# Second-layer modulation summed on VectorE, and the convolution branch ahead of the gating branch

## The chip, the cores and the metric

The kernel runs on one core of a Trainium2 chip. Its time is device microseconds of one execution. Three executions took 2710.41 us in the median (2707.55 to 2712.38).

## What is computed

Two transformer blocks follow each other, both with two layers, 256 tokens of width 1024, all in float32.

Part 1, per layer: a mixer with three attention branches (each gated by a sigmoid and projected, then summed), a layer norm, cross attention to a memory of 256 rows, a layer norm, a SwiGLU feed-forward network (FFN) of width 2816, a layer norm.

Part 2, per layer, works on those 256 tokens and, in its first layer, on 256 context tokens beside them. Its modulation and the merge of its branches are, cut from the reference:

```python
silu_c, silu_cc = jax.nn.silu(c), jax.nn.silu(c_ctx)            # one vector of 1024 each
mod_lat = (silu_c @ ada_w[l] + ada_b[l])[:, None, :]            # ada_w[l]: 1024 x 6144
mod_ctx = silu_cc @ ada_w[l] + ada_b[l]
sh1, sc1, g1, sh2, sc2, g2 = jnp.split(mod_lat, 6, axis=-1)
csh1, csc1, cg1, csh2, csc2, cg2 = jnp.split(mod_ctx, 6, axis=-1)
h = modulate(rmsnorm(x, norm1_g[l]), sh1, sc1)                  # also for the context
z = h @ w_in[l]
y_a = spatial_gating(gelu(z_u), layernorm(gelu(z_v)))           # gating branch
y_b = rmsnorm(differential_attention(z_q, z_k, z_v))            # attention branch
y_c = gb * dwconv3(gc * xin, cw)                                # convolution branch
m = g_a * (y_a @ wa) + g_b * (y_b @ wb) + g_c * (y_c @ wc)      # g: sigmoid gates of h
x = x + g1 * (m @ wo)
x = x + g2 * conv_ffn(modulate(rmsnorm(x, norm2_g[l]), sh2, sc2))
```

In the last layer only the keys and values of the context are used, so of the context's modulation only `csh1` and `csc1` (the first 2048 columns) count there.

## The kernel before

Each weight matrix is split into a high and a low part, and a product takes three matmuls (high by high, high by low, low by high). `wload` (line 83) fetches 512 KB of weights by SP's queue into one of three `raw` tiles; ScalarE writes the high part into one of four `whi` tiles (L91), VectorE the low part into one of four `wlo` tiles (L92). `gemm_N` (line 100) streams 512 weight columns against 128 tokens at a time, matmuls L96 to L98; `gemm_T` (line 141) streams the tokens, matmuls L171. Accumulators of both come from four PSUM banks (`acc_g`); two more (`acc_m`) serve transposes and small products, and one pair (`acc_s`) the attention scores.

The program is written as Python loops that are unrolled. A planner orders each engine's instructions when the kernel is built: it takes the earliest instruction in program order that its own cost estimates hold for ready, with a tile free for it. Later work is thus moved into gaps of earlier work, and each engine then runs its list strictly as laid out. SP holds all loads and stores in one list. `behind` (line 76) adds order to that: while `fence["D"]` is set, the conversions on VectorE come after the fenced instruction. `post_norm` sets it to the last operation of the norm behind cross attention (`ln_xa_g`, line 421), whose function also calls a `filler` between the norm and the transposes of its result (line 423).

Modulation: `ada_steps` (line 684) computes both streams of both layers of part 2 in 48 steps, three groups of 2048 columns per layer and eight steps of 128 rows per group. A step loads two raw tiles of 512 KB (no conversion) and issues four float32 matmuls of 32 columns by 512 (L696), which appear as eight records; a group ends with the addition of the bias on VectorE (L704) and stores to DRAM (`modd`), from where `mod_row` reads single rows later. Of the 48 steps, 8 are the filler of the norm behind cross attention in each layer of part 1, 8 that of the norm behind the first FFN; 11 stand in each FFN's loop, one per iteration (line 817), and one behind each FFN (line 840). The filler of the norm behind the mixer is `mem_k`, the key projection of the memory (96 matmuls L171). Tiles of the ring `kv_tile` (8 of 512 KB) serve keys, values and modulation weights.

Part 2, per layer: key, value and query GEMMs; eight attention heads in two groups of four (scores L1046, transposes L347, products L1067, transposes of keys and queries L1024); the GEMM of the gating values with `emit_sv` (line 1120), which takes the slot `mT` for its result `sv`; `gating` with its own products (L1142); `merge(0)`, which begins the sum `mT`; `head_norm`, which scales the attention output; `convolution`; `merge(2)`; then, in memory that the attention released, the transposes of the attention output and `merge(1)`. In layer 1 the convolution stands before `merge(0)`. In layer 0 the tile tags double: keys and queries of heads 0 to 3 use the slot of `mT`, those of heads 4 to 7 the slot `y` of the branch results.

Of the kernel before, what the change touches and what calls it, by code (L numbers as in the profile page):

```python
# [12 lines left out]
ALU = mybir.AluOpType  # L13
# [14 lines left out]
def body(ctx: ExitStack, tc: tile.TileContext, A: dict, out: bass.AP):  # L28
# [12 lines left out]
    cfg = {"narrow": True, "pt": 3}  # L41
# [31 lines left out]
    def v3(ap, n):  # L73
        return ap.rearrange("p (a b) -> p a b", b=n)
# [8 lines left out]
    def wload(kt, n, srcs):  # L83
# [8 lines left out]
        behind("D", V.tensor_sub(lo[:, :kt * n], raw[:, :kt * n], hi[:, :kt * n]))  # L92
        return v3(hi[:, :kt * n], n), v3(lo[:, :kt * n], n)
# [128 lines left out]
    ident = cst.tile([128, 128], F32, name="ident")  # L222

# [43 lines left out]
    def kv_tile():  # L267
        return xo.tile([128, 1024], F32, name="kv", tag="kv", bufs=8)
# [385 lines left out]
    def mem_k(l):  # L654
        kx = v3(kv_tile(), 256)
        evac_T(kx, gemm_T(memT, 256, A["xa_w_kv"][l], 0, 4))
        return kx
# [13 lines left out]
    def ada_prep():  # L671
# [40 lines left out]
    def ada(n, P, raw_tile):  # L712
        cfg["ada"] = (P, raw_tile)
        for _ in range(n):
            next(ada_it)

# [46 lines left out]

    for l in range(L):
        mfin = mixer(l, xT)
        with tc.tile_pool(name="xa", bufs=1, reuse_waits="tile") as P:
            mem = {}

            def fill_k(l=l):
                mem["k"] = mem_k(l)  # L770
            x, xT = post_norm(P, pair(mfin), A["w_mix_out"][l], 8, x, "ln_mix_g", "ln_mix_b", l, filler=fill_k)
            kx = mem["k"]
# [24 lines left out]
            for qb in range(2):  # L797
                ops = v3(bank_m(), 128)
                for h in range(4):
                    for kt in range(2):  # L800
# [5 lines left out]
                              filler=lambda: ada(8, P, lambda: P.tile([128, 1024], F32, name="adar", tag="adar", bufs=8)))  # L806
        with tc.tile_pool(name="ffn", bufs=1, reuse_waits="tile") as P:
# [4 lines left out]
            for (cb, nb, gps), (_, _, ups) in zip(gg, uu):  # L812
# [4 lines left out]
                ada(1, P, kv_tile)  # L817
# [22 lines left out]
            ada(1, P, kv_tile)  # L840
# [12 lines left out]
    cfg.update(narrow=False, pt=2)  # L853
    def md_tile(P):
        return lambda: P.tile([128, 1024], F32, name="md", tag="md", bufs=7)
# [32 lines left out]
    for l in range(L):  # L888
# [7 lines left out]
        with tc.tile_pool(name="mix2", bufs=1, reuse_waits="tile") as P:  # L896
# [220 lines left out]

            sv = P.tile([128, 4, 512], F32, name="sv", tag="mT", bufs=1)

            def emit_sv(tb, ps):  # L1120
                gv = gelu2(ps)
                st = small()[:, :6]
                mv = small()[:, :2]
                V.bn_stats(out=st, in_=gv)
                V.bn_aggr(out=mv, in_=st)
                rs = rsqrt(mv[:, 1:2], 1, 1.0, 4e-6)
                V.tensor_scalar(out=sv[:, tb, :], in0=gv, scalar1=mv[:, 0:1], scalar2=rs, op0=ALU.subtract, op1=ALU.mult)
            gemm_N(hT, qtbs, W, 512, 512, emit_sv, tail=2)

# [3 lines left out]
            def gating():  # L1133
# [18 lines left out]
            def merge(n, y, Wb, kt):  # L1152
                proj = gemm_T(y, ntok, Wb, 0, 8, kt=kt)
                gate = gemm_T(hT, ntok, W, 5632 + n * 1024, 8)
                for (cb, nb, gps), (_, _, pps) in zip(gate, proj):
# [3 lines left out]
                    if n == 0:  # L1159
# [42 lines left out]
            with tc.tile_pool(name="yb", bufs=1, reuse_waits="tile") as PB:  # L1202
                yb = PB.tile([128, 2, 8, ntok], F32R, name="yb", tag="yb")
                for tb in qtbs:
# [7 lines left out]
                merge(1, pair(yb), A["w_br_b_2"][l], 8)  # L1212
            mfin = wide_xT()
            for cb in range(8):
                split((mfin[0][:, cb, 0:ntok], mfin[1][:, cb, 0:ntok]), mT[:, cb, :], scale=0.5)
        with tc.tile_pool(name="ffn2", bufs=1, reuse_waits="tile") as P:
# [24 lines left out]
            for npart in ((12, 10) if ns == 2 else (22,)):  # L1241
# [6 lines left out]
                for (cb, nb, gps), (_, _, ups) in zip(gg, uu):  # L1248
# [8 lines left out]
            if l == 0:  # L1257
                hT2 = modulated(P, 1, (1, 0), "norm1_g_2", 0)

# [58 lines left out]
```

## Time and profile before

| | |
|---|---|
| median of three executions | 2710.41 us (2707.55 to 2712.38) |
| profiled execution | 2707.87 us, span 2706.1 us |
| TensorE (PE) matmuls | busy 2639.3 us, 98% |
| VectorE (DVE) | busy 1698.3 us, 63% |
| ScalarE (ACT) | busy 1245.0 us, 46% |
| mean granted TensorE clock | 0.991 of full |
| DMA | 419.16 MB, mean 155 GB/s |

A busy TensorE isn't TensorE at its peak: its matmuls are pipelined and the ends of records are modelled, so neighbouring records overlap, and what one costs is read from the distance between starts. The granted clock is the mean over a stretch of a clock with two levels. A line number such as L92 is that of the listing; where a helper issues an instruction, the line is the helper's. Part 1 runs from 0 to about 1160 us, layer 0 of part 2 to about 2145 us, layer 1 to the end.

### The profile page before, as it was taken

The numbers are of one execution on the slowest core, as the hardware profiler recorded it, in microseconds if no ns is written. First come the engines' busy times: TensorE is split into PE (matmuls) and PEld (weight loads), VectorE is DVE, ScalarE is ACT, GpSimd is POOL, SyncE is SP. The second block draws the span as 40 slices with busy tenths as digits, with TensorE's granted clock in tenths as the row PEclk, the third lists the DMA queues.
The fourth block names the chain that finished last, engine by engine and source line by source line (L and its number), as shares of the span: only waits on it lengthen the run. The fifth ranks groups of instructions, "written<-read, shape, count | busy, mean of one in ns | idle before, by whom it ended". The sixth has DMA issues, their size and how long they took to land.

```text
span 2706.1 us, 40562 instructions
## 1 busy us (share of the span) xinstructions
PE 2639.3 (98%) x15961; PEld 2238.6 (83%) x15961; DVE 1698.3 (63%) x3227; ACT 1245.0 (46%) x1983; POOL 24.6 (1%) x12
## 2 busy tenths in 40 slices
PE   9999999999999999999989999999999999999999
PEld 8889879868988698777767888788888877899997
DVE  6666754546666656678656433675365787766884
ACT  5655434326554444346653222344143356644663
POOL 0010000000010000000000000000000000000000
PEclk9999999999999999999989999999999999999999
DMA  7545877765457687531112333443232233366564
GB/s 223 159 133 179 279 265 244 237 209 161 141 158 265 228 277 244 184 97 55 55 55 71 101 94 94 157 130 96 86 117 93 84 103 108 110 190 208 169 185 153
DMA packets 416838, 419.16 MB, mean 155 GB/s; under 512 B 19708, under 2 KB 348760, under 8 KB 416648
## 3 DMA queue, kind: packets, MB, share of 16 engines
q1 hardware_dynamic: 416648, 416.58, 49.1%
q8 instruction: 125, 2.05, 0.3%
q14 instruction: 65, 0.53, 0.1%
HBM read 415.36 MB, written 1.16 MB: 154 GB/s over the span
## 4 chain that ended last, share of the span: by engine, by line
PE 87%; DVE 6%; ACT 3%; DMA 2%; issue 1%; POOL 0%; POOLq 0%; SPq 0%; ACTq 0%; DVEq 0%
PE acc_g L171 50%; PE acc_g L98 9%; PE acc_g L96 9%; PE acc_g L97 9%; PE acc_m L696 2%; PE acc_m L347 2%; DVE wlo L92 1%; PE acc_m L1067 1%; ACT whi L91 1%; PE acc_s L1046 1%; PE acc_m L378 1%; ACT ap L1057 1%; DVE ap L1062 1%; PE acc_m L231 0%; PE acc_s L471 0%
## 5 line engine op out<-in xcount | busy, mean ns | idle before, releaser
L92 DVE TENSOR_TENSOR wlo<-raw,whi 128x1024 fp32r<-128x1024 f32 (+3 forms) x644 | 782.2, 1216 | 642.5 <-ACT whi L91 635.8
L171 PE MATMUL acc_g<-xT,whi 128*128 128x256 f32 (+1 forms) x5440 | 1165.8, 311 | 1.6 <-ACT xT L209 1.2
L91 ACT CAST whi<-raw 128x1024 fp32r<-128x1024 f32 (+3 forms) x644 | 667.6, 1038 | 924.3 <-PE acc_g L171 499.7
L171 PEld LDWEIGHTS acc_g<-xT,whi 128*128 128x128 f32 x5440 | 882.5, 189 | 85.5 <-issue 23.4
L171 PE MATMUL acc_g<-xT,wlo 128*128 128x256 f32 (+1 forms) x2720 | 836.5, 310 | 0.0
L171 PEld LDWEIGHTS acc_g<-xT,wlo 128*128 128x128 f32 x2720 | 511.3, 189 | 30.0 <-issue 2.1
L96 PE MATMUL acc_g<-whi,xT 128*128 128x512 f32 (+2 forms) x792 | 313.4, 397 | 0.9 <-ACT xT L209 0.7
L98 PE MATMUL acc_g<-whi,xT 128*128 128x512 f32 (+2 forms) x792 | 312.6, 395 | 0.0
L97 PE MATMUL acc_g<-wlo,xT 128*128 128x512 f32 (+2 forms) x792 | 312.5, 395 | 0.0
L96 PEld LDWEIGHTS acc_g<-whi,xT 128*128 128x128 f32 x792 | 150.3, 190 | 35.7 <-issue 4.7
L98 PEld LDWEIGHTS acc_g<-whi,xT 128*128 128x128 f32 x792 | 150.4, 190 | 33.6 <-issue 5.1
L97 PEld LDWEIGHTS acc_g<-wlo,xT 128*128 128x128 f32 x792 | 150.5, 190 | 32.1 <-issue 4.4
L171 PE MATMUL acc_g<-y,whi 128*128 128x256 f32 (+1 forms) x640 | 135.4, 305 | 0.2 <-ACT y L212 0.2
L171 PEld LDWEIGHTS acc_g<-y,whi 128*128 128x128 f32 x640 | 102.8, 188 | 7.0 <-ACT y L212 0.9
L97 PE MATMUL acc_g<-wlo,hid 128*128 128x512 f32 x264 | 104.3, 395 | 0.0
L98 PE MATMUL acc_g<-whi,hid 128*128 128x512 f32 x264 | 104.3, 395 | 0.0
L96 PE MATMUL acc_g<-whi,hid 128*128 128x512 f32 x264 | 104.3, 395 | 0.0
L171 PE MATMUL acc_g<-y,wlo 128*128 128x256 f32 (+1 forms) x320 | 97.4, 304 | 0.0
L349 ACT COPY pt<-acc_m 128x512 f32<-128x512 f32 (+1 forms) x92 | 50.3, 547 | 62.6 <-PE acc_m L347 62.3
L1057 ACT ACTIVATE ap<-acc_s,sa,rq 128x512 f32<-128x512 f32 (+1 forms) x96 | 67.2, 706 | 20.4 <-DVE sa L1054 20.3
L96 PE MATMUL acc_g<-whi,hT 128*128 128x512 f32 x176 | 69.8, 397 | 0.0
L97 PE MATMUL acc_g<-wlo,hT 128*128 128x512 f32 x176 | 69.5, 395 | 0.0
(325 smaller groups left out, 2929.9 us busy)
## 6 DMA issues: line engine op xcount, KB each, us to landing
raw<-in_w_in_dram SPq DMA_DIRECT2D x200, 512.0 KB
raw<-in_ffn_w_gu_dram SPq DMA_DIRECT2D x88, 512.0 KB
raw<-in_ffn_up_dram SPq DMA_DIRECT2D x88, 512.0 KB
kv<-in_ada_w_dram SPq DMA_DIRECT2D x64, 512.0 KB
raw<-in_ffn_w_down_dram SPq DMA_DIRECT2D x44, 512.0 KB
raw<-in_ffn_down_dram SPq DMA_DIRECT2D x44, 512.0 KB
adar<-in_ada_w_dram SPq DMA_DIRECT2D x32, 512.0 KB
raw<-in_w_in_dram SPq DMA_DIRECT2D x64, 256.0 KB
```

The costliest lines, as they stand in the source:

```text
L91: behind("A", SC.copy(hi[:, :kt * n], raw[:, :kt * n]))
L92: behind("D", V.tensor_sub(lo[:, :kt * n], raw[:, :kt * n], hi[:, :kt * n]))
L96: PE.matmul(acc, sh, mh, start=first, stop=False)
L97: PE.matmul(acc, sh, ml, start=False, stop=False)
L98: PE.matmul(acc, sl, mh, start=False, stop=last)
L171: PE.matmul(acc[:, j, cut], blocks[kk][wi], xT[xi][:, kk, cut], start=n == 0, stop=n == len(steps) - 1)
L347: PE.transpose(p3[:, j, :], s2d[:, j * 128:(j + 1) * 128], ident)
L349: SC.copy(pt[:, :n * 128], ps[:, :n * 128])
L378: PE.matmul(ops[64 * e:64 * e + 64, i, :], pv(hsets[e][i], kt), pts[e][:, i * nkt + kt, :], start=kt == 0, stop=kt == nkt - 1)
L696: PE.matmul(acc[32 * j:32 * j + 32, :], scT[:, k, :], raw[:, jj * 512:(jj + 1) * 512], start=k == 0, stop=k == 7)
L1046: PE.matmul(pss[a_], QT[r, qi, tb * 128:tb * 128 + 128], KT[r, ki, k0:512], start=i == 0, stop=i == 2)
L1057: SC.activation(out=p[a_], in_=pss[a_], func=AF.Exp, scale=rq[tb][:, a_, h:h + 1], bias=nm[:, a_:a_ + 1], accum_out=sums[:, a_:a_ + 1])
```

## The change

1. `ada_steps` runs over layer 0 of part 2 alone: 24 steps. The calls `ada(1, ...)` in and behind the FFNs go. The fillers are: `mem_k(0)`, then `mem_k(1)` behind cross attention in layer 0 (its result in another tile, `xc`), 8 steps behind the FFN of layer 0, 8 steps behind the mixer of layer 1, 8 steps behind its cross attention.
2. Layer 1's modulation is computed by the new generator `ada_last` during layer 0 of part 2. It advances by one step every second `wload` (`cfg["rate"]` = 0.5) in the merges and gating, and in the FFN. A step loads 512 KB into a tile of the ring `raw`, multiplies it by the condition value of its row (per partition), and adds it to a 128x1024 accumulator, all on VectorE: four operations of 128x512 where both streams are needed (first 2048 columns, two row blocks per step), one of 128x1024 elsewhere (one row block per step). After 4 or 8 steps, 48 in all, the chunk is split into high and low, summed over the partitions by four matmuls against a matrix with one column of ones, copied by ScalarE and stored.
3. In part 2 the order is convolution, `merge(2)`, `head_norm`, release of the attention's memory, gating (its value GEMM included, `sv` now in that memory), `merge(0)`, transposes, `merge(1)`.

```diff
@@ wload
+        cfg["due"] += cfg["rate"]
+        if cfg["due"] >= 1:
+            cfg["due"] -= 1
+            next(ada_l1, None)
         return v3(hi[:, :kt * n], n), v3(lo[:, :kt * n], n)
@@ mem_k
-        kx = v3(kv_tile(), 256)
+        kx = v3(kv_tile() if l == 0 else xc.tile([128, 1024], F32, name="xc", tag="xc", bufs=2), 256)
@@ ada_prep
+        V.tensor_copy(cond, scT[:, :, 0:2])
+        zo = xo.tile([128, 129], F32, name="zo")
+        V.memset(zo, 0.0)
+        V.memset(zo[:, 1:2], 1.0)
+        SC.copy(pick, zo)
@@ ada_steps
-        for l in range(L):
+        for l in (0,):
@@ new
+    def ada_last():
+        W = A["ada_w_2"][1]
+        bias = A["ada_b_2"][1:2]
+        for c0 in (0, 512, 1024, 1536, 2048, 3072, 4096, 5120):
+            both = c0 < 2048
+            acc = cfg["acc"]()
+            V.memset(acc, 0.0)
+            for j in range(2):
+                c = c0 if both else c0 + 512 * j
+                nc.sync.dma_start(out=acc[0:1, j, :], in_=bias[:, c:c + 512])
+            for k in range(0, 8, 2 if both else 1):
+                raw = wp.tile([128, 1024], F32, name="raw", tag="raw", bufs=3)
+                if both:
+                    nc.sync.dma_start(out=v3(raw, 512), in_=W[k * 128:(k + 2) * 128, c0:c0 + 512].rearrange("(k p) n -> p k n", p=128))
+                    for kk in range(2):
+                        for s in range(2):
+                            V.scalar_tensor_tensor(out=acc[:, s, :], in0=raw[:, kk * 512:kk * 512 + 512],
+                                                   scalar=cond[:, k + kk, s:s + 1], in1=acc[:, s, :], op0=ALU.mult, op1=ALU.add)
+                else:
+                    nc.sync.dma_start(out=raw, in_=W[k * 128:(k + 1) * 128, c0:c0 + 1024])
+                    a2 = acc.rearrange("p a b -> p (a b)")
+                    V.scalar_tensor_tensor(out=a2, in0=raw, scalar=cond[:, k, 0:1], in1=a2, op0=ALU.mult, op1=ALU.add)
+                if k < (6 if both else 7):
+                    yield
+            hi = v3(wp.tile([128, 1024], F32R, name="whi", tag="whi", bufs=4), 512)
+            lo = v3(wp.tile([128, 1024], F32R, name="wlo", tag="wlo", bufs=4), 512)
+            SC.copy(hi, acc)
+            V.tensor_sub(lo, acc, hi)
+            ps = bank_m()
+            for j in range(2):
+                for i, part in enumerate((hi, lo)):
+                    PE.matmul(ps, pick[:, 1 - j:129 - j], part[:, j, :], start=j + i == 0, stop=j + i == 2)
+            SC.copy(acc[0:2, 0, :], ps[0:2, :])
+            dst = modd[1, :, c0:c0 + 512] if both else modd[1, 0:1, c0:c0 + 1024].rearrange("o (j n) -> (o j) n", j=2)
+            nc.sync.dma_start(out=dst, in_=acc[0:2, 0, :])
+            yield
@@ part 1, each layer
-            x, xT = post_norm(P, pair(mfin), A["w_mix_out"][l], 8, x, "ln_mix_g", "ln_mix_b", l, filler=fill_k)
+            x, xT = post_norm(P, pair(mfin), A["w_mix_out"][l], 8, x, "ln_mix_g", "ln_mix_b", l,
+                              filler=(lambda: fill_k(0)) if l == 0 else lambda: ada(8, P, kv_tile))
...
-                              filler=lambda: ada(8, P, lambda: P.tile([128, 1024], F32, name="adar", tag="adar", bufs=8)))
+                              filler=(lambda: fill_k(1)) if l == 0 else lambda: ada(8, P, adar_tile))
...
-                ada(1, P, kv_tile)
...
-            ada(1, P, kv_tile)
@@ part 2, each layer (gating now holds emit_sv and its GEMM, with sv = PB.tile(...))
-            ya = gating()
             mT = P.tile([128, 8, ntok], F32, name="mT", tag="mT", bufs=1)
-            if ns == 1:
-                yc = convolution()
-            merge(0, pair(ya), A["w_br_a_2"][l], 4)
+            yc = convolution()
+            if l == 0:
+                cfg["rate"] = 0.5
+            merge(2, pair(yc), A["w_br_c_2"][l], 4)
             for tb in qtbs:
                 head_norm(tb)
-            if ns == 2:
-                yc = convolution()
-            merge(2, pair(yc), A["w_br_c_2"][l], 4)
             att.close()
             with tc.tile_pool(name="yb", bufs=1, reuse_waits="tile") as PB:
                 yb = PB.tile([128, 2, 8, ntok], F32R, name="yb", tag="yb")
+                ya = gating(PB)
+                merge(0, pair(ya), A["w_br_a_2"][l], 4)
...
                 merge(1, pair(yb), A["w_br_b_2"][l], 8)
+            cfg["rate"] = 0
@@ FFN of part 2, in the loop over hidden blocks
+                    if l == 0:
+                        cfg["rate"] = 0.5
...
+                if b0 > 0:
+                    cfg["rate"] = 0
```

The first merge to run (now `merge(2)`) writes `mT`, the others add to it.

## Rows read from the trace of the kernel before

**Rows 1.** Page: engine, busy us, share of the span, instructions
```profile
PE 2639.3 (98%) x15961; PEld 2238.6 (83%) x15961; DVE 1698.3 (63%) x3227; ACT 1245.0 (46%) x1983; POOL 24.6 (1%) x12
```

**Rows 2.** Windows: length; busy PE, PEld, DVE, ACT, POOL; clock; DMA share; GB/s
```profile
1400.00:1420.00 20.00, 13.18 (x57) 9.93 (x58) 7.69 (x22) 9.62 (x24) 0.00 (x0) 0.56 0.00 0
1560.00:1580.00 20.00, 20.00 (x88) 16.28 (x87) 7.94 (x9) 5.62 (x7) 0.00 (x0) 1.00 0.26 80
2340.00:2360.00 20.00, 16.49 (x125) 16.27 (x126) 14.61 (x30) 11.74 (x21) 0.00 (x0) 0.91 0.16 44
```

**Rows 3.** Chain of waits, attention of layer 0: start, us, what
```profile
1380.22 0.44 PE acc_s L1024 x4
...
1383.41 3.92 PE acc_g L171 x16
1387.34 0.55 PE acc_s L1046 x5
```

**Rows 4.** Windows of line 696: length; busy PE, PEld; clock; DMA; GB/s
```profile
364.00:500.00 136.00, 11.72 (x88) 1.73 (x88) 1.00 0.77 252
560.00:600.00 40.00, 15.89 (x72) 2.36 (x72) 0.91 0.73 250
937.80:1075.00 137.20, 8.57 (x66) 1.25 (x62) 1.00 0.81 265
```

**Rows 5.** Chain of waits, two FFN iterations of part 1
```profile
373.38 11.58 PE acc_g L171 x96
385.95 11.59 PE acc_g L171 x96
```

**Rows 6.** Lines: operation, tiles, count | busy us, mean ns | idle before
```profile
L92 DVE TENSOR_TENSOR wlo<-raw,whi 128x1024 fp32r<-128x1024 f32 (+3 forms) x644 | 782.2, 1216 | 642.5 <-ACT whi L91 635.8 <-PE acc_g L171 4.3
...
L1109 DVE SCALAR_TENSOR_TENSOR sp<-sp 128x512 f32<-128x512 f32 x12 | 8.2, 686 | 0.3
...
L704 DVE TENSOR_TENSOR ab<-ab,acc_m 128x512 f32<-128x512 f32 x6 | 4.1, 684 | 5.6 <-PE acc_m L696 5.5
```

**Rows 7.** Chain of waits, neighbouring matmuls of 128x512
```profile
560.08 0.24 PE acc_g L96
560.32 0.23 PE acc_g L97
```

**Rows 8.** Waits of ScalarE, 1440 to 2130: us, times, longest
```profile
ACT whi L91 <- DMA raw<-in_ffn_up_dram: 3.6, 2, 2.7
```

**Rows 9.** Timeline, norm behind cross attention, layer 0: start, us, what
```profile
352.54 1.41 DVE L400 SCALAR_TENSOR_TENSOR x<-x,sm,ln 128x512 f32<-128x512 f32 x2
...
354.06 0.66 PE L231 MATMUL acc_m<-ident,x 128*128 128x128 f32 x4
...
358.86 0.50 PE L171 MATMUL acc_g<-xT,whi 128*128 128x256 f32 x2
...
360.59 1.05 PE L696 MATMUL acc_m<-adar,scT 128*32 128x512 f32 x4
```

**Rows 10.** Windows at the first norm of layer 0 and of layer 1
```profile
280.00:300.00 20.00, 19.83 (x141) 18.40 (x140) 18.80 (x42) 7.62 (x9) 0.00 (x0) 1.00 0.93 322
870.00:880.00 10.00, 7.71 (x29) 5.88 (x28) 4.25 (x5) 3.55 (x5) 0.00 (x0) 0.83 0.77 287
```

**Rows 11.** Chain of waits at three norms of part 1
```profile
294.36 4.34 PE acc_g L171 x34
...
345.83 3.79 DMA adar<-in_ada_w_dram
...
864.10 7.42 DMA raw<-in_xa_w_q_dram
```

**Rows 12.** Windows of line 347, of line 1067, and of all instructions
```profile
1345.00:1392.50 47.50, 3.67 (x22) 2.44 (x22) 1.00 0.23 67
...
1345.00:1392.50 47.50, 6.22 (x44) 5.63 (x44) 1.00 0.23 67
...
1392.50:1426.70 34.20, 22.96 (x111) 17.21 (x109) 17.39 (x43) 20.84 (x47) 0.00 (x0) 0.70 0.05 16
```

More of the change, by code (lines that the diff above doesn't have):

```diff
@@ L40, in body @@
     SP2 = 4
-    cfg = {"narrow": True, "pt": 3}
+    cfg = {"narrow": True, "pt": 3, "rate": 0, "due": 0}
     fence = {}
@@ L222, in body @@
     ident = cst.tile([128, 128], F32, name="ident")
+    pick = cst.tile([128, 129], F32R, name="pick")
+    cond = cst.tile([128, 8, 2], F32, name="cond")
     def to_T(nat, dst, tb, ks=(0, 4), tag="m"):
@@ L715, in ada @@
             next(ada_it)
+    def ada_last():
[34 more added lines that the diff above has]
+            yield
+    ada_l1 = ada_last()
     ssq = {}
@@ L762, in modulate @@
         return h
+    mem = {}
     for l in range(L):
@@ L766, in body, with adar_tile, fill_k @@
         with tc.tile_pool(name="xa", bufs=1, reuse_waits="tile") as P:
-            mem = {}
-            def fill_k(l=l):
-                mem["k"] = mem_k(l)
-            x, xT = post_norm(P, pair(mfin), A["w_mix_out"][l], 8, x, "ln_mix_g", "ln_mix_b", l, filler=fill_k)
-            kx = mem["k"]
+            def adar_tile():
+                return P.tile([128, 1024], F32, name="adar", tag="adar", bufs=8)
+            def fill_k(n):
+                mem[n] = mem_k(n)
+            x, xT = post_norm(P, pair(mfin), A["w_mix_out"][l], 8, x, "ln_mix_g", "ln_mix_b", l,
+                              filler=(lambda: fill_k(0)) if l == 0 else lambda: ada(8, P, kv_tile))
+            kx = mem[l]
             qx = v3(kv_tile(), 256)
@@ L853, in body @@
     cfg.update(narrow=False, pt=2)
+    ad = ExitStack()
+    PD = ad.enter_context(tc.tile_pool(name="ad", bufs=1))
+    cfg["acc"] = lambda: PD.tile([128, 2, 512], F32, name="ada", tag="ada", bufs=1)
     def md_tile(P):
@@ L1115, in flat, with gating, emit_sv @@
                 return ps.rearrange("p a b -> p (a b)")
[L1118 to L1128, printed above, removed]
             def y_tile():
                 return P.tile([128, 2, 4, ntok], F32R, name="y", tag="y", bufs=3 - ns)
-            def gating():
+            def gating(PB):
+                sv = PB.tile([128, 2 * ns, 512], F32, name="sv", tag="sv")
+                def emit_sv(tb, ps):
+                    gv = gelu2(ps)
+                    st = small()[:, :6]
+                    mv = small()[:, :2]
+                    V.bn_stats(out=st, in_=gv)
+                    V.bn_aggr(out=mv, in_=st)
+                    rs = rsqrt(mv[:, 1:2], 1, 1.0, 4e-6)
+                    V.tensor_scalar(out=sv[:, tb, :], in0=gv, scalar1=mv[:, 0:1], scalar2=rs, op0=ALU.subtract, op1=ALU.mult)
+                gemm_N(hT, qtbs, W, 512, 512, emit_sv, tail=2)
                 ya = y_tile()
@@ L1158, in merge @@
                     m = flat(mT[:, cb:cb + nb, :])
-                    if n == 0:
+                    if n == 2:
                         V.scalar_tensor_tensor(out=m, in0=g, scalar=1.0, in1=flat(pps), op0=ALU.add, op1=ALU.mult)
@@ L1257, in body @@
             if l == 0:
+                for _ in ada_l1:
+                    pass
                 hT2 = modulated(P, 1, (1, 0), "norm1_g_2", 0)
+        if l == 0:
+            ad.close()
 _INS = [
```

## Prediction

> **What bounds the kernel now.** I read the page's busy times first: TensorE is busy for 2639.3 of 2706.1 us, that is 98% [rows 1]. A change is therefore worth the TensorE time that it takes away or fills, and the 67 us of TensorE idle time only where they lie. Windows over the span then show where that is: almost everywhere TensorE is full at a granted clock of 1.00; the exceptions are the layer norms of part 1 and the end of each attention of part 2. The worst stretch is 1400 to 1420 us: busy 13.18 of 20 us at a clock of 0.56, with the DMA queues at 0 [rows 2]. A share of 0.56 is mostly the lower of the two levels (1.2 of 2.4 GHz), so even the busy part there runs at about half speed. Last, I took the chain of waits for the cadence of the loops, and the timelines around the norms.
>
> The engines' order is not the program's: a planner lays it out at build time and takes later work that is ready. Sixteen matmuls of the U GEMM (L171) run between attention matmuls (L1024, L1046) at 1383 us [rows 3]. So work that stands later in the program fills earlier gaps, as far as tiles are free.
>
> **The change, part by part.**
>
> *Modulation steps leave part 1.* A step is four logical matmuls, shown as 8 records (L696). Before there are 48 steps, after 24. The three fillers of 8 steps stay (one moves), so what goes are the 24 steps in and behind the two FFNs. In layer 0, the window 364 to 500 holds 88 records, 11 steps, with 11.72 us busy [rows 4]. On the path they cost less: an FFN iteration is 11.59 us of GEMM, repeated every 12.59 us, so 1.00 us each [rows 5]: 11.0 us. The twelfth runs inside 560 to 600 (72 records are 9 steps, 8 of them the filler): about 1 us. In layer 1, 937.8 to 1075 shows 66 records, 8.57 us [rows 4]; the other 22 of its FFN's 88 records already fill the norm ahead of it and give nothing back. The last step stands in the gap before a norm; only its addition on VectorE (L704, 0.68 us each [rows 6]) goes from the norm's chain. Sum: 11.0 + 1.0 + 8.6 + 0.7 = 21.3 us saved. Nothing is late in its place: the iteration's 4 weight tiles cost VectorE 4 x 1.216 us [rows 6], far under 11.59.
>
> *They come back in part 2, layer 0.* TensorE gets 8 chunks x 4 = 32 matmuls of 128x512. Neighbouring matmuls of that shape follow each other by 0.23 us [rows 7]: 32 x 0.23 = 7.4 us on the path, plus about 1 us, an estimate, for places where TensorE meets `lo` too early: +8.5 us. VectorE gets 64 operations of 128x512 at 0.686 us (44 us), and 32 of 128x1024, which the trace doesn't have; the nearest is L92 at 1.216 us (39 us) [rows 6]; with 8 memsets, 8 subtractions and the waits between them some 100 us in all, over 48 steps, one per two weight tiles, over more than 600 us. In that stretch VectorE is busy 7.94 of 20 us while TensorE is full [rows 2], so I cost it at nothing; what hides it is that a weight tile feeds 24 matmuls of 0.23 us (5.6 us) and four converted ones can stand ready. Gone that cover, it costs up to the full 100 us. ScalarE gets 8 conversions more, hidden likewise. On SP 48 loads of 512 KB move from the FFNs to here, into the queue and the three `raw` tiles of the weights; in this stretch ScalarE waits for a landing only 3.6 us in all [rows 8].
>
> *Three fillers change places.* (a) The norm behind cross attention in layer 0 had 8 modulation steps, and gets the K projection of layer 1. Its conversions on VectorE are held by `fence["D"]` behind the norm's last operation (L400 x2, ends 352.54 + 1.41 = 353.95) [rows 9], which raw modulation weights never were. TensorE is then empty from about 345 but for the transposes of the first half; the first `lo` is ready at 353.95 + 1.22 = 355.2; 96 matmuls take 11.6 us [rows 5], the last transposes 2 x 0.66 [rows 9]: FFN from 368.1. Before, it starts at 358.86 and still loses two half steps of about 1.2 us: 361.2 [rows 9]. Cost: 6.9 us (bounds 0, if the order hides it all, and 12).
>
> (b) The first norm of layer 0 loses the DMA load of the 8 `adar` tiles: there the DMA share is 0.93 [rows 10], and K matmuls that wait for weights (34 in 4.34 us) are on the chain itself [rows 11]. I take 2 us gained (0 to 4).
>
> (c) The first norm of layer 1 swaps the K projection for 8 steps. Before, its chain waits 7.42 us for a w_q tile [rows 11] and TensorE runs 7.71 of 10 us at a clock of 0.83 [rows 10]. Without the K weights, w_q can be in place earlier: 5 us gained; the second half of the 16 `kv` tiles must wait for released ones, and modulation steps have waited 3.79 us for tiles before [rows 11]: 2 us lost. I take 3 gained (8 gained to 6 lost). Together: +2 us.
>
> In (a) the clock is a further matter. Rows first: after the idle time before 875 us the granted clock is 0.83 over 10 us. The Trainium skill (TensorE: Matmul & The Clock Gate, Part 1) says that an array left idle falls to half rate and returns only with sustained work. By that rule the K projection would start at the lower level, and (a) would cost what such a stretch cost at 870 us, 3.4 us at half level or 1.7 us, more; by the rows alone it is 6.9.
>
> *The convolution goes first.* The last head's K and Q are transposed at 1380.22 (L1024) [rows 3]; from about 1392.5 to 1426.7 (34.2 us) the filler has run out: `sv` holds the slot of `mT`, and gating's own matmuls (L1142) stand behind the heads. That window holds 111 matmul records. In the undisturbed window before it such records took 3.67/22 = 0.17 us (L347) and 6.22/44 = 0.14 us (L1067) [rows 12]; at 0.15 they are 16.6 us of work, and 17.6 us are lost. With the change, ready work there is 12 convolution GEMMs (24 x 0.23 = 5.6 us each, 67 us) and, since `mT` is free, merge 2 behind them; `yc` takes the slot of K and Q after 1380. Against some 50 us of filler before, it doesn't run out. Gain 17.6 us (0 if the filler isn't taken up, 21 if the heads also run without gaps). Layer 1 shows the same, smaller: 3.5 us idle in 2340 to 2360 and a clock of 0.91 over 20 us [rows 2], which is 3.6 us at half level and costs 1.8: I take 5 of 5.3.
>
> Gating now stands alone between merges, with no heads beside it. Its chain, 4 gelus with statistics, then 4 more with products, is some 32 us of VectorE (0.69 us each [rows 6]), with weight tiles and steps 50 us, against U and about three gates of cover (7 x 5.6 = 39 us) behind its first results. I take 4 us lost in layer 0 and 1 in layer 1 (0 to 17: all that the attention hid). `head_norm` moves behind merge 2 with the same cover as now.
>
> **Sum.** -21.3 + 8.5 + 2 - 17.6 - 5 + 5 = -28.4 us. The profiled execution took 2707.87 us (its span and 1.8 around it), which gives 2679.5; it lies 2.5 under the median of the runs shown (2710.41), so I forecast 2681 against that median.
>
> **Rivals.**
> 1. *The filler moves, but the gap moves with it*: gating without heads beside it stalls for all that it won (17 instead of 4), and layer 1 gives nothing: 2681 + 13 + 5 = 2699. For: two alternations of ScalarE and VectorE per gelu. Against: gates need only `hT`, and U and gates are ready.
> 2. *All is covered*: no loss in (a), none in gating, (c) at its best: 2681 - 7 - 5 - 5 = 2664. For: the planner interleaves freely. Against: the fence.
> 3. *DMA in part 1*: the `kv` tiles of (c) start as soon as slots are free, in layer 1's mixer, beside the bias broadcasts and w_q, at a DMA share that is 0.93 already: (c) costs 6 instead of gaining 3, and the mixer 3: 2693.
> 4. *Slower: a landing holds VectorE.* A modulation operation waits directly on its DMA; `wlo` stands behind it. Two weight tiles give TensorE 11.2 us; two `wlo` (2.4) and a step (2.8) leave 6.0. Landings under that cost nothing. At a wait of 7.42 us, as w_q showed, each of the 48 steps loses 1.4 us once the four ready tiles are used: +68 us, 2749. Against: 0.26 DMA share there [rows 2]. It decides from a wait of 6.0 us; slower than before from 6.6 (48 x 0.6). By the Trainium skill (the same page, on the array of 16 sub-arrays) ScalarE and VectorE take their queues strictly in order; VectorE's idle time before `wlo` in these rows, all of it on ScalarE, doesn't contradict it.
>
> **How the numbers follow.** Forecast (2670 to 2690) 0.52; rival 1 0.14; rival 2 0.14; rival 3 0.12; rival 4 0.08. The range 2662 to 2701 holds the first four but for their edges. What this kernel's measurement can tell from no change is 0.2%, 5.4 us: faster 0.86 (of the cases but rival 4, less a tail in which several losses meet), same 0.06, slower 0.08.
>
> **What would show it.** FFN iterations of part 1 at 11.6 us without L696 between; 192 L696 records; conversions of the K projection after L400 in layer 0 and TensorE nearly empty in front of them; no window at a clock near 0.56 at the end of the heads, convolution GEMMs between L1046 and L1067 there; 32 new matmuls beside full TensorE in 1400 to 2100, and VectorE near 11 of 20 us. It is wrong if TensorE has gaps with releaser `wlo` in part 2's merges, or if gating shows a gap above 10 us.

## The result

The changed kernel takes 2672.32 us (median of 4 runs, 2671.67 to 2673.55), the kernel before, run beside it, 2711.39 (2707.55 to 2712.72). The ratio is 0.9857, with a 95% interval of 0.9843 to 0.9872: 39 us faster. The forecast was 28.4 us faster, 2681 in a range of 2662 to 2701; the time lies inside the range and 9 us under the forecast. Of the profiled executions the span fell from 2706.1 to 2669.9 us, by 36.2.

### The profile page after: what moved, and what is told of

Its sections match the earlier page's. It is cut to its first block, busy times and chain, and to the rows that moved or that the text cites. A ratio compares the mean times of both kernels' runs of the same rounds, so it can differ in the third digit from the quotient of the medians.

```text
span 2669.9 us, 40432 instructions
## 1 busy us (share of the span) xinstructions
PE 2613.1 (98%) x15801; PEld 2232.9 (84%) x15801; DVE 1793.8 (67%) x3339; ACT 1258.4 (47%) x2000; POOL 24.3 (1%) x12
## 4 chain that ended last, share of the span: by engine, by line
PE 88%; DVE 6%; ACT 2%; DMA 2%; issue 1%; SPq 0%; DVEq 0%; ACTq 0%
PE acc_g L175 50%; PE acc_g L102 9%; PE acc_g L101 9%; PE acc_g L100 9%; DVE wlo L92 2%; PE acc_m L354 2%; PE acc_m L1127 1%; PE acc_s L1106 1%; PE acc_m L708 1%; ACT whi L91 1%; DMA raw<-in_w_in_dram 1%; PE acc_m L385 1%; PE acc_m L238 1%; PE acc_s L478 0%; PE acc_s L1084 0%
## 5 line engine op out<-in xcount | busy, mean ns | idle before, releaser
L175 PE MATMUL acc_g<-xT,whi 128*128 128x256 f32 (+1 forms) x5440 | 1166.5, 311 | 0.9 <-ACT xT L213 0.5
L92 DVE TENSOR_TENSOR wlo<-raw,whi 128x1024 fp32r<-128x1024 f32 (+2 forms) x644 | 785.9, 1222 | 507.7 <-ACT whi L91 504.8
L91 ACT CAST whi<-raw 128x1024 fp32r<-128x1024 f32 (+2 forms) x644 | 667.7, 1038 | 825.1 <-PE acc_g L175 410.5
L175 PEld LDWEIGHTS acc_g<-xT,whi 128*128 128x128 f32 x5440 | 882.1, 189 | 65.7 <-issue 8.5
L175 PE MATMUL acc_g<-xT,wlo 128*128 128x256 f32 (+1 forms) x2720 | 838.5, 310 | 0.3 <-DVE wlo L92 0.3
L175 PEld LDWEIGHTS acc_g<-xT,wlo 128*128 128x128 f32 x2720 | 511.8, 189 | 30.5 <-issue 3.1
L100 PE MATMUL acc_g<-whi,xT 128*128 128x512 f32 (+2 forms) x792 | 311.8, 395 | 0.9 <-ACT xT L213 0.7
L102 PE MATMUL acc_g<-whi,xT 128*128 128x512 f32 (+2 forms) x792 | 311.1, 393 | 0.0
L100 PEld LDWEIGHTS acc_g<-whi,xT 128*128 128x128 f32 x792 | 149.8, 189 | 36.1 <-issue 4.7
L102 PEld LDWEIGHTS acc_g<-whi,xT 128*128 128x128 f32 x792 | 149.8, 189 | 31.3 <-issue 2.7
L175 PE MATMUL acc_g<-y,whi 128*128 128x256 f32 (+1 forms) x640 | 135.2, 305 | 0.0
L175 PEld LDWEIGHTS acc_g<-y,whi 128*128 128x128 f32 x640 | 103.0, 188 | 6.2 <-issue 0.7
L102 PE MATMUL acc_g<-whi,hid 128*128 128x512 f32 x264 | 104.3, 395 | 0.0
L100 PE MATMUL acc_g<-whi,hid 128*128 128x512 f32 x264 | 104.3, 395 | 0.0
L175 PE MATMUL acc_g<-y,wlo 128*128 128x256 f32 (+1 forms) x320 | 97.0, 303 | 0.0
L100 PE MATMUL acc_g<-whi,hT 128*128 128x512 f32 x176 | 69.3, 394 | 0.0
```

The costliest lines, as they stand in the source:

```text
L91: behind("A", SC.copy(hi[:, :kt * n], raw[:, :kt * n]))
L100: PE.matmul(acc, sh, mh, start=first, stop=False)
L102: PE.matmul(acc, sl, mh, start=False, stop=last)
L175: PE.matmul(acc[:, j, cut], blocks[kk][wi], xT[xi][:, kk, cut], start=n == 0, stop=n == len(steps) - 1)
```

## The profile after

Line numbers have moved: a weight tile's conversions are still L91 and L92, the GEMMs L175 (was L171) and L100 to L102 (L96 to L98), the modulation matmul L708 (L696), the norm's last operation L407 (L400), the FFN's Silu L873 (L814), the new matmuls of the modulation L765, its operations on VectorE L750 and L755. First the page's busy times, which answer to [rows 1]:

```profile
PE 2613.1 (98%) x15801; PEld 2232.9 (84%) x15801; DVE 1793.8 (67%) x3339; ACT 1258.4 (47%) x2000; POOL 24.3 (1%) x12
```

TensorE has 192 instructions of the modulation fewer and 32 more, and is busy for 26 us less; the other 10 us of the span were idle time. VectorE has 95 us more to do, as forecast. The windows over the end of layer 0's heads and over the gating that follows (columns as in [rows 2]):

```profile
1380.00:1400.00 20.00, 20.00 (x110) 15.53 (x111) 15.53 (x34) 12.12 (x26) 0.00 (x0) 1.00 0.34 103
1400.00:1420.00 20.00, 20.00 (x88) 16.27 (x87) 19.31 (x57) 8.32 (x13) 0.00 (x0) 1.00 0.44 132
1480.00:1500.00 20.00, 20.00 (x88) 16.19 (x87) 18.67 (x44) 10.69 (x18) 0.00 (x0) 1.00 0.41 119
1500.00:1520.00 20.00, 20.00 (x103) 16.78 (x103) 19.11 (x45) 8.70 (x13) 0.00 (x0) 1.00 0.48 144
```

The stretch at a clock of 0.56 [rows 2] is gone. VectorE's work of gating begins at 1483 us; VectorE is nearly full there, TensorE quite. In between, one chunk of the modulation as the timeline of TensorE has it (start, us, what), and what VectorE waited for in 1430 to 2020 us (us in total, times, longest):

```profile
1438.56 0.40 PE L765 MATMUL acc_m<-whi,pick 128*128 128x512 f32 x1
1438.80 0.39 PE L765 MATMUL acc_m<-wlo,pick 128*128 128x512 f32 x1
1439.03 0.39 PE L765 MATMUL acc_m<-whi,pick 128*128 128x512 f32 x1
1439.26 0.40 PE L765 MATMUL acc_m<-wlo,pick 128*128 128x512 f32 x1
```

```profile
DVE wlo L92 <- ACT whi L91: 90.8, 51, 5.9
DVE ada L755 <- DMA raw<-in_ada_w_dram: 30.5, 19, 4.0
...
DVE ada L750 <- DMA raw<-in_ada_w_dram: 4.3, 1, 4.3
```

The matmuls follow each other by 0.23 us, as [rows 7] said. VectorE does wait for landings, 20 times in these operations, but never for more than 4.3 us. In one place the profile has become worse, the norm behind cross attention in layer 0 (windows, then rows of the timelines of VectorE and TensorE; against [rows 9]):

```profile
340.00:345.00 5.00, 3.50 (x18) 2.73 (x16) 4.61 (x13) 1.05 (x1) 0.00 (x0) 1.00 0.44 166
345.00:350.00 5.00, 1.35 (x5) 0.95 (x6) 4.90 (x20) 0.59 (x1) 0.00 (x0) 0.58 0.00 0
350.00:355.00 5.00, 4.80 (x22) 4.26 (x22) 4.96 (x7) 1.76 (x3) 0.00 (x0) 0.50 0.18 51
```

```profile
350.18 1.41 DVE L407 SCALAR_TENSOR_TENSOR x<-x,sm,ln 128x512 f32<-128x512 f32 x2
351.52 3.49 DVE L92 TENSOR_TENSOR wlo<-raw,whi 128x1024 fp32r<-128x1024 f32 x3
```

```profile
351.08 1.94 PE L238 MATMUL acc_m<-ident,x 128*128 128x128 f32 x8 [0.20 <-DVE x L407]
...
352.79 0.58 PE L175 MATMUL acc_g<-memT,wlo 128*128 128x256 f32 x1
...
365.32 0.40 PE L175 MATMUL acc_g<-xT,whi 128*128 128x256 f32 x2
```

The conversions stand behind the norm's last operation, TensorE is nearly empty in front of them, and the FFN starts at 365.3 us.

To see where time goes, one takes the same instruction in both traces and subtracts its starts. This is the whole account, in us against the kernel before, for the changed kernel and for three of the experiments below (worked out from the timelines, each from one profiled execution):

```
start before, what                        after  e1_order  e2_modul  e6_oldfill
 298.1  last L400, first norm, layer 0     -1.3    -0.4      -1.7      -1.3
 353.2  last L400, cross attention, l. 0   -2.4    -0.3      -3.0      -1.8
 555.2  last but one addition, FFN, l. 0   -8.4    -0.3     -10.1     -13.5
 575.9  last L400, FFN, layer 0            -9.3    -3.4     -10.9     -18.2
 844.5  first addition, first norm, l. 1   -8.5    -3.6     -10.9     -18.9
 931.4  last L400, cross attention, l. 1  -14.3    -3.2     -16.6     -23.3
1134.4  last addition of part 1           -19.6    -3.2     -21.9     -31.3
1242.0  first head of part 2              -19.9    -1.8     -22.5     -30.6
1716.5  last merge of layer 0             -35.0   -20.9     -14.0     -45.3
2221.6  first head of layer 1             -31.3   -20.9     -10.8     -41.9
2482.1  last merge of layer 1             -36.4   -26.1     -10.8     -47.2
2702.3  last addition                     -36.2   -24.0      -9.8     -45.3
```

The column of e1_order also shows how exact such an account is: part 1 of that kernel is the one of before, and still 3.1 us went between 555 and 576, and 2.1 came back behind layer 1's last merge. The 3.1 us go with the granted clock, which was lower for a while in the one execution and not in the other (the kernel before, then e1_order):

```profile
560.00:580.00 20.00, 16.37 (x74) 6.21 (x72) 12.01 (x28) 2.70 (x4) 0.00 (x0) 0.83 0.61 211
```

```profile
560.00:580.00 20.00, 17.17 (x87) 7.14 (x86) 12.40 (x29) 2.98 (x5) 0.00 (x0) 1.00 0.72 253
```

The changed kernel, e2_modul, e5_double, e7_twice and e9_last have the same part 1, instruction for instruction, and its last addition starts at 1114.8, 1112.5, 1117.2, 1112.6 and 1111.9 us in them. So differences of 3 us in a stretch, and of 5 us over part 1, can be chance.

## The experiments

Each was timed beside the kernel before, which took 2708.9 to 2709.0 us (medians) in these runs. The changed kernel was not run again beside them, and the kernel before took 2.5 us more beside it. So what is said below against its 2672.32 us is sure to some 2.5 us: by the ratios, e3_unheld would be 6.0 and e6_oldfill 6.8 us faster than the changed kernel, e5_double 11.1, e7_twice 13.8 and e9_last 2.4 slower.

**The order alone** (e1_order): part 2's hunks of the diff without the lines on `rate`, everything else as before.

```diff
-            ya = gating()
             mT = P.tile([128, 8, ntok], F32, name="mT", tag="mT", bufs=1)
...
+            yc = convolution()
+            merge(2, pair(yc), A["w_br_c_2"][l], 4)
...
+                ya = gating(PB)
+                merge(0, pair(ya), A["w_br_a_2"][l], 4)
```

> The kernel before, with the order of part 2 alone changed: convolution and merge 2 ahead of gating and merge 0; all 48 modulation steps stay in part 1. Theory A (the order closes the gap at the ends of the heads, gating alone costs nothing because U, gates and proj cover it): 20 us from layer 0 and 5 from layer 1, so 25 under the kernel before, 2686 us (2682 to 2690). Theory B (the prediction's working: gating then loses 5 of it again): 17.6 under, 2694. Theory C (the gap closes only together with the modulation work, which gives TensorE and VectorE other things to do there): under 10, above 2700.

Measured: 2682.98 us against 2708.88, ratio 0.9906 (0.9892 to 0.9919), 25.9 faster. Theory A. The account gives 19.1 us to layer 0 (-1.8 to -20.9) and 5.2 to layer 1. Its window at the end of the heads:

```profile
1400.00:1420.00 20.00, 20.00 (x109) 15.56 (x108) 13.97 (x38) 15.27 (x32) 0.00 (x0) 1.00 0.17 54
```

So the gap closes without any modulation work in it. From 1380 to 2130 us TensorE waits for 0.7 us in all, so gating costs nothing there. The edit moves two things at once, the convolution ahead and `sv` out of the slot of `mT`; which of them lets the filler through isn't tested.

**The modulation alone** (e2_modul): the changed kernel with part 2's branch order of before, `rate` set behind gating.

```diff
-            yc = convolution()
+            ya = gating()
             if l == 0:
                 cfg["rate"] = 0.5
...
+            merge(0, pair(ya), A["w_br_a_2"][l], 4)
...
```

> The changed kernel with the branch order of before in part 2 (gating first); modulation of layer 1 on VectorE and the three fillers as in the change. Theory A (parts add up): -20 for the FFN steps, +7.5 for 32 new matmuls, +1 for the fillers: 12 under the kernel before, 2699 us (2696 to 2703), and the stretch at the lower clock near the end of layer 0's heads is back. Theory C (the parts help each other: the new VectorE work needs the convolution first, beside gating it delays the weight conversions): above 2705. Theory D (modulation work costs nothing at all in part 2): 20 under, 2691.

Measured: 2698.11 us, ratio 0.9961 (0.9949 to 0.9974), 10.8 faster; theory A. The gap at the heads is back:

```profile
1360.00:1380.00 20.00, 15.68 (x77) 10.60 (x75) 11.96 (x27) 9.64 (x22) 0.00 (x0) 0.84 0.34 104
1380.00:1400.00 20.00, 13.03 (x53) 9.44 (x54) 7.78 (x22) 10.21 (x25) 0.00 (x0) 0.50 0.00 0
```

Of its own, the modulation costs 11.7 us in part 2 here (-22.5 to -10.8), and 7.7 in the changed kernel (layer 0 gains 11.4 there, -19.9 to -31.3, where the order alone gains 19.1). That doesn't show that the modulation is 4 us cheaper with the convolution first: 3.3 of the 4 us are lost here from 1313 to 1420 us (the starts of L1069, an operation of the heads, go from -22.5 to -19.2), in the gap itself, where the granted clock is lower still than before (e2_modul, then the kernel before):

```profile
1340.00:1440.00 100.00, 87.88 (x414) 67.09 (x413) 73.27 (x189) 50.36 (x101) 0.00 (x0) 0.85 0.21 66
```

```profile
1340.00:1440.00 100.00, 88.28 (x448) 66.61 (x446) 69.75 (x187) 63.40 (x131) 0.00 (x0) 0.90 0.14 43
```

The first steps on VectorE run there already, from 1342 us; whether they make the gap longer or chance does isn't settled. As sums, 25.9 and 10.8 make 36.7; the changed kernel is 36.6 under the 2708.9 of these runs, so nothing is left that the two parts would do only together.

**The fillers on the kernel before** (e4_fill), and **the fillers of before in the changed kernel** (e6_oldfill), the same edit in both directions; here the second:

```diff
-        kx = v3(kv_tile() if l == 0 else xc.tile([128, 1024], F32, name="xc", tag="xc", bufs=2), 256)
+        kx = v3(kv_tile(), 256)
-                              filler=(lambda: fill_k(0)) if l == 0 else lambda: ada(8, P, kv_tile))
+                              filler=lambda l=l: fill_k(l))
-                              filler=(lambda: fill_k(1)) if l == 0 else lambda: ada(8, P, adar_tile))
+                              filler=lambda: ada(8, P, adar_tile))
```

> The kernel before, with only the three fillers moved as in the change; the other 24 steps stay in the FFNs and the order of part 2 stays. The prediction's term: +2 (+6.9 for the norm behind cross attention in layer 0, -2 and -3 for the first norms). The anchors of the two traces: +6 there, -2 at the first norm, -1 in the net of layer 1's mixer and first norm: 2713 us (2710 to 2717). Rival 3 of the prediction (tiles loaded early crowd the mixer of layer 1): +11, 2722. Rival 2: -5 to -12, below 2707.

> The changed kernel with the three fillers where they were before (K projections in both first norms, modulation steps in both norms behind cross attention). Theory A (the moved fillers cost 5.5 us in layer 0's norm behind cross attention and 2.4 in layer 1's mixer, and win 1 at the first norm of layer 0 and 1 at that of layer 1, by the anchors of the traces): 6 under the changed kernel, 2666 us (2663 to 2669). The prediction's own term: 2 under, 2670. Rival (their cost is the +9 that they had on the kernel before): 2663 or less.

Measured: the fillers alone make the kernel before slower, 2718.16 us, ratio 1.0034 (1.0021 to 1.0047), 9.3 more. Taken out of the changed kernel they give 2663.64 us (2662.53 to 2664.48), ratio 0.9832 (0.9817 to 0.9846), 8.7 under the changed kernel. Both directions agree; my figures from starts in the two traces (the anchors of the expectations: 3 in the first, 6 in the second) were too small. 2663.64 us lies at the low end of theory A's range and 0.6 above the rival's bound, so the second run alone doesn't decide between them; with the first, it is nearer to the rival's 9. The first run's sum is near rival 3's +11, but most of it isn't lost in rival 3's place: in its account 5.6 us go between the norm behind cross attention and the end of the FFN in layer 0, 1.8 in layer 1's mixer. Against e6_oldfill the changed kernel loses 5.7 us from cross attention to the end of layer 0's FFN (-6.0 against -11.7), nothing at layer 0's first norm, 1.5 in layer 1's mixer, and from 844 to 1134 us 1.3 (-11.1 against -12.4). The 3.8 between 555 and 576 us can't be told from what e1_order shows there by chance, nor can the 1.5 in the mixer: in the five kernels with the same part 1 the stretch from 576 to 844 us takes between 268.3 and 272.8 us.

What [rows 11] have as a wait of 7.42 us for a w_q tile isn't the filler's either. What ScalarE waited for around layer 1's first norm, in e1_order and in e6_oldfill:

```profile
ACT whi L91 <- DMA raw<-in_xa_w_q_dram: 8.8, 3, 6.8
```

```profile
ACT whi L91 <- DMA raw<-in_xa_w_q_dram: 1.4, 3, 0.9
```

Both have the K projection there. The wait is nearly gone where the FFN's modulation steps are gone; SP issues the same loads in the same order in both there, so why the landing is earlier isn't settled, and one execution alone shows it.

**The K projection not held** (e3_unheld): the one filler that follows `fence["D"]` is issued ahead of it.

```diff
-        if want_T and gname == "ln_xa_g":
+        held = want_T and gname == "ln_xa_g"
+        if held and l > 0:
             fence["D"] = cfg["ln"]
         if filler is not None:
             filler()
+        if held:
+            fence["D"] = cfg["ln"]
```

> The changed kernel, but the K projection that fills layer 0's norm behind cross attention isn't held behind the norm's last operation. Theory A (the hold costs what the trace shows: TensorE has 5.4 us idle in 340 to 355 us and runs 9 us at the lower level behind it): 6 us under the changed kernel, 2666 us (2664 to 2669), the window 345 to 350 filled and the granted clock 1.00 there. Rival: the four conversions (4 x 1.22 us) push the norm's own chain on VectorE back by as much, so the FFN starts no earlier: 2671 to 2674.

Measured: 2664.11 us (2663.46 to 2666.25), ratio 0.9835 (0.9822 to 0.9849), 8.2 under the changed kernel. Theory A; the norm's windows, then the FFN's first row without a gap behind it:

```profile
345.00:350.00 5.00, 5.00 (x44) 5.00 (x43) 4.96 (x14) 1.05 (x1) 0.00 (x0) 1.00 0.80 259
350.00:355.00 5.00, 5.00 (x44) 5.00 (x44) 4.89 (x15) 2.11 (x2) 0.00 (x0) 1.00 0.66 234
```

```profile
357.66 0.39 PE L175 MATMUL acc_g<-xT,whi 128*128 128x256 f32 x1
```

The rival's half is true too: the norm's last operation starts 3.1 us later than in the changed kernel, at 353.92 against 350.85 us. The FFN still starts 7.7 us earlier, 357.66 against 365.32, since the 11.6 us of K matmuls now lie beside that chain.

**Twice the work on VectorE** (e5_double) and **twice the loads** (e7_twice), both for the cover that the prediction counted on.

```diff
-                    V.scalar_tensor_tensor(out=a2, in0=raw, scalar=cond[:, k, 0:1], in1=a2, op0=ALU.mult, op1=ALU.add)
+                    for _ in range(2):
+                        V.scalar_tensor_tensor(out=a2, in0=raw, scalar=cond[:, k, 0:1], in1=a2, op0=ALU.mult, op1=ALU.add)
```

```diff
-                    nc.sync.dma_start(out=raw, in_=W[k * 128:(k + 1) * 128, c0:c0 + 1024])
+                    for _ in range(2):
+                        nc.sync.dma_start(out=raw, in_=W[k * 128:(k + 1) * 128, c0:c0 + 1024])
```

(and so in the chunks of two rows).

> The changed kernel with each of the modulation's 96 multiply-adds on VectorE made twice, so layer 1's modulation values come out doubled: 64 x 0.686 + 32 x about 1.2 = 82 us more on VectorE between 1430 and 2010 us, on 2672. Theory A (VectorE's part lies under TensorE's weight tiles with room to spare): 0 to 4 more, 2672 to 2676, TensorE still at 20.00 of 20 us there. Rival 4 of the prediction, in its form for time on VectorE (the conversions stand behind these operations in order and TensorE waits for them): 20 to 60 more, 2692 to 2732.

> The changed kernel with each of the 48 loads of layer 1's modulation weights made twice into the same tile (24 MB more, the operation that reads it starts after the second). Theory A (landings come under their cover): 0 to 3 more, 2672 to 2675. Rival 4 of the prediction (a landing holds VectorE, and the weight conversions behind it): over 15 more, above 2687, with TensorE waiting for wlo in the merges.

Measured: 2681.80 us (ratio 0.9898, 0.9881 to 0.9914) and 2683.68 (0.9908, 0.9893 to 0.9922), 9.5 and 11.4 more than the changed kernel. Each is over theory A and under rival 4, the doubled work far under its 20 to 60, the doubled loads not far under its 15: the cover holds nearly everywhere and is thin at a few places. For the doubled work it is mostly one place, the gating. Its window, and what TensorE waited for in it:

```profile
1520.00:1540.00 20.00, 15.22 (x68) 11.60 (x67) 20.00 (x30) 9.11 (x14) 0.00 (x0) 1.00 0.33 102
```

```profile
PE acc_g L175 <- DVE wlo L92: 4.8, 2, 3.8
```

VectorE is full, and the weights' `wlo` comes late, which is rival 4's chain with time on VectorE in place of a landing. For the doubled loads the windows are these, and for the first two of them what the engines waited for:

```profile
1460.00:1480.00 20.00, 17.96 (x77) 14.04 (x75) 9.70 (x13) 4.59 (x5) 0.00 (x0) 1.00 0.52 158
1500.00:1520.00 20.00, 16.03 (x72) 12.40 (x71) 15.09 (x41) 5.66 (x8) 0.00 (x0) 0.98 0.64 198
1600.00:1620.00 20.00, 17.84 (x75) 13.90 (x73) 10.09 (x11) 6.48 (x9) 0.00 (x0) 0.91 0.50 157
```

```profile
ACT whi L762 <- DVE ada L751: 10.6, 1, 10.6
DVE ada L751 <- DMA raw<-in_ada_w_dram: 10.2, 2, 6.4
...
PE acc_m L767 <- ACT whi L762: 1.4, 1, 1.4
```

```profile
ACT whi L91 <- DMA raw<-in_w_in_dram: 10.0, 2, 8.1
...
PE acc_m L1203 <- DVE sv L1193: 3.7, 2, 2.2
```

Here the longest wait of VectorE for a landing is 6.4 us, just above the 6.0 from which rival 4 was to decide, against 4.3 in the changed kernel. What stops TensorE isn't a `wlo` of the weights, though: it is a chunk's closing matmul (L767 here), which stands in TensorE's order and waits for a sum that waits for a load; in 1500 to 1520 it is gating's matmuls, which wait for `sv` (3.7 us). There `sv` stands on VectorE behind a `wlo` whose own weights land late: ScalarE waits 8.1 us for them. Their load stands in SP's list behind a pair of doubled ones, of which the second waits in that list until the first has landed (at L755 here, 102.1 us in 40 times from 1430 to 2030 us). So this run does more than double the bytes, it also holds the loads of the weights.

**Gating behind everything** (e9_last): gating and merge 0 behind merge 1.

```diff
-                ya = gating(PB)
-                merge(0, pair(ya), A["w_br_a_2"][l], 4)
...
                 merge(1, pair(yb), A["w_br_b_2"][l], 8)
+                ya = gating(PB)
+                merge(0, pair(ya), A["w_br_a_2"][l], 4)
```

> The changed kernel with gating and merge 0 moved once more, behind merge 1: nothing but gating's own GEMMs, the gates of merge 0 and the modulation steps is left to cover its chain on VectorE. Theory A (gating costs nothing in the changed kernel because merge 1 stands behind it and is taken earlier): layer 0 loses 4 to 12 us and layer 1 3 to 10, since there half the tokens give half the GEMM time; 2679 to 2694 us. Rival, the prediction's account (U and about three gates are the cover, whatever stands behind): no more is lost than now, 2672 to 2675.

Measured: 2672.00 us (2670.62 to 2675.26), ratio 0.9866 (0.9849 to 0.9882): no difference, the rival. Two waits of TensorE are all that gating leaves there:

```profile
1599.40 0.71 PE L1201 MATMUL acc_m<-wsT,sv 128*128 128x128 f32 x4 [0.81 <-DVE sv L1191]
1603.48 0.71 PE L1201 MATMUL acc_m<-wsT,sv 128*128 128x128 f32 x4 [0.57 <-DVE sv L1191]
```

So its own GEMMs, U and the gates, are cover enough; merge 1 isn't needed for it.

**Other tiles for layer 1's steps** (e8_own): e3_unheld with `ada(8, P, adar_tile)` in place of `ada(8, P, kv_tile)` in layer 1's first norm.

> The unheld version (2664) with the modulation steps of layer 1's first norm in the eight tiles that the norm behind cross attention has, so that their loads can't start inside the mixer. Theory A (the loads in the mixer cost 2.4 us there, and the norm then waits for some of 4 MB in 12 us): the mixer wins 2, the norm loses 0 to 6: 2662 to 2668, 2665. Rival (SP's queue and the DMA weigh on nothing in the mixer): the mixer stays, 2667 or more.

Measured: 2668.01 us (2665.47 to 2669.17), ratio 0.9847 (0.9832 to 0.9861), 3.9 more than e3_unheld. Up to 844 us it wins 3.1 us (-17.1 against -14.0), of which 0.9 lie ahead of the mixer; the other 2.2 are within what equal mixers differ by. From there to the end of cross attention 5.7 are lost. What TensorE and ScalarE waited for in 820 to 920 us:

```profile
PE acc_m L711 <- DMA adar<-in_ada_w_dram: 2.2, 5, 0.9
```

```profile
ACT whi L91 <- DMA raw<-in_xa_w_q_dram: 10.6, 4, 6.9
```

e3_unheld shows neither wait there. The time lies where theory A's upper end and the rival's lower end meet, so it doesn't decide whether the loads cost anything in the mixer. Moved out of it, they cost 4 us more than they give.

The fastest version of these is the change without its moved fillers, e6_oldfill, at 2663.6 us, 45 under the kernel before; e3_unheld is as fast (2664.1).

## Why the prediction was right, and by how much each step was off

*Modulation steps leave part 1: -21.3.* With the fillers held as before (e6_oldfill), layer 0's FFN gives 11.7 us (11.0 forecast), layer 1's 8.0 (9.3 with L704), and the stretch from layer 1's first norm to the norm behind cross attention another 4.4: the w_q wait, which I had booked under the move of filler (c), goes with the FFN's steps. That step gained about 25 us (11.7 + 8.0 + 4.4, and 1 at the norm behind layer 0's FFN, once the 3.4 us that the lower clock cost the kernel before there are taken off).

*Modulation in part 2: +8.5.* Measured 7.7, as worked out under e2_modul. The matmuls are 32 x 0.23 = 7.4; the 1 us added for TensorE meeting `lo` too early didn't come. VectorE at nothing was right for this kernel, with less room than I gave it: a window I had read at 7.94 of 20 us [rows 2] isn't where the modulation meets gating, at 18 to 19 of 20.

*Fillers: +2.* Measured +8.7, the worst miss. (a) was read rightly: the FFN starts 4.1 us later than the 361.2 of before, from a norm that ends 2.4 earlier, so 6.5 against 6.9 (half steps of 1.05 us, as [rows 9] have it, in place of 1.2 would make it 361.0), of which the account keeps 5.7 at the FFN's end. The granted clock came beside it: after the idle time it is 0.58 and 0.50 in the windows above, and the 14 K matmuls behind it, which step by 0.21 us there and by 0.12 later, took some 1.3 us more. By the Trainium skill (TensorE: Matmul & The Clock Gate, Part 1) an idle array falls to half rate; the trace agrees. The prediction had 1.7 us for that in case. That the sum came out without it is luck: the last transposes, 1.3 us behind the K projection in the prediction, ran ahead of it (at 351.08).

(b) gave 0 of 2: from its first addition to its last operation the norm takes 23.4 us in the kernel before, the changed one and e6_oldfill. I had misread its row: 34 matmuls in 4.34 us [rows 11] are 0.128 us each, where 96 in 11.6 [rows 5] are 0.121, so they hardly waited for weights. (c) did make its norm shorter, 21.4 us against 23.8 in e6_oldfill, but 1.5 went in the mixer ahead of it and 3.7 behind it up to the end of part 1, so about 3 were lost where 3 were to be gained. Rival 3 had the mixer lose 3; the 1.5 is within chance, and its cause isn't shown.

*The convolution first: -17.6 and -5.* Measured 19.1 and 5.2, together with gating's cost, which TensorE's waits put at nothing. The gap closes wholly, as its upper bound of 21 allowed; the filler didn't run out.

*Gating standing alone: +5.* Measured 0. The cover that the prediction named, U and the gates, is real and enough; 50 us of chain against 39 us of cover was the wrong comparison. The changed kernel's rows (VectorE, TensorE, TensorE, VectorE):

```profile
1483.42 0.69 DVE L1169 SCALAR_TENSOR_TENSOR sp<-sp 128x512 f32<-128x512 f32 x1
```

```profile
1490.51 0.63 PE L175 MATMUL acc_g<-xT,whi 128*128 128x512 f32 x2
...
1521.96 0.63 PE L175 MATMUL acc_g<-y,whi 128*128 128x512 f32 x2
```

```profile
1528.03 0.69 DVE L217 SCALAR_TENSOR_TENSOR y<-sp,y 128x512 fp32r<-128x512 f32 x1
```

The chain begins 7 us before gating's first GEMM ends (1490.51), and merge 0 takes the first part of `y` from 1521.96 us, before the last one is made (1528.03). What U and the gates have to cover is the 31 us between, not 50. Rival 1 falls with it.

So four terms were too cautious (by 4, 1, 2 and 5 us) and one, the fillers, was 7 too hopeful; together they make 33 of the 36.2 us of the span, and the rest is of the size that an execution shows by chance. That the total came out within 9 us is in part these misses taking each other off. The step that failed is the move of the fillers: its sum had a credit in (b) that no run shows, and one in (c) that was more than lost again around the norm. *Rival 2* had gating right; its (a) at nothing needs the hold lifted, and e3_unheld, at 2664.1 us, then meets its 2664, though not by its (c).

*Rival 4* didn't come in the changed kernel, where VectorE's longest wait for a landing is 4.3 us and TensorE waits for no `wlo`. With the loads doubled, VectorE waits for 32 landings from 1430 to 2030 us, one of them for more than 6.0 (6.4), and the run costs 11 us and not 68. But its chain isn't the rival's: no wait of TensorE there is for a weight's `wlo`. So one landing over the bound agrees with 6.0 and doesn't test it. The prediction's reading of VectorE's idle time beside it was a little off, too: in [rows 6] 635.8 of the 642.5 us before `wlo` are on ScalarE, not all.

## What to carry to other kernels

A gap at the end of a serial chain closed here when the work behind it needed nothing that the chain held; ask which tile keeps later work out, and put first the branch that needs neither that tile nor a free slot (that it was the tile is read from the program's order, no run moves it alone). A filler is only worth its place if its own first operations aren't held behind the chain that it should cover: a few lines on the fence were worth 8 us (6 by the ratios). When one change has several parts, run each alone and in reverse: here a part that lost 9 us was hidden in a gain of 39.

## What the runs showed of the hardware

Work on GpSimd went with slower work on VectorE. In layer 1's mixer of the changed kernel, a weight conversion that takes 1.22 us elsewhere takes 4.50 beside GpSimd's additions (timeline of GpSimd, then of VectorE):

```profile
738.33 3.61 POOL L617 TENSOR_TENSOR bias<-bias,Fq 128x2048 f32<-128x2048 f32 x1
742.01 3.20 POOL L620 TENSOR_TENSOR bias<-bias,cmask 128x1024 f32<-128x1024 f32 x1
```

```profile
738.52 4.50 DVE L92 TENSOR_TENSOR wlo<-raw,whi 128x1024 fp32r<-128x1024 f32 x1 [2.39 <-ACT whi L91]
742.94 0.68 DVE L636 SCALAR_TENSOR_TENSOR mT<-g,acc_g 128x512 f32<-128x512 f32 x1
743.54 2.76 DVE L92 TENSOR_TENSOR wlo<-raw,whi 128x1024 fp32r<-128x1024 f32 x1
```

The operation between them, with an operand in `acc_g`, keeps its 0.68 us. By the Trainium skill (SBUF — State Buffer, Who interferes with whom) a VectorE instruction with two SBUF inputs contends with a GpSimd instruction that reads SBUF, and one with at most one SBUF input, outside its two-port modes, doesn't; the conversion reads `raw` and `whi`, the operation between reads one operand from PSUM, so these rows agree. No run here takes GpSimd's work away.

The multiply-adds that the trace of before didn't have take 746 ns for 128x512 and 1283 ns for 128x1024 in the mean; 686 and 1216 had been taken for them.
